# Turning the next expert's rows during the second matrix, in single buffers, with more weight pieces in flight

## The chip, the core and the metric

The kernel runs on one core of one Trainium2 chip. The metric is device time in microseconds (us) of one execution. TensorE (PE) multiplies matrices, VectorE (DVE) and ScalarE (ACT) work elementwise, GpSimd (POOL) issues indirect transfers, and SyncE (SP) issues nearly all the loads of weights. Each engine takes its instructions in the order of its own list.

## What is computed

One decoder layer on 1024 tokens of width 1024. The first third of the time goes to attention and cross-attention; the rest, which the change touches, is the mixture of experts. The router picks 4 of 32 experts for each token, and each expert does this to its tokens:

```python
gu = xb @ w1[e] + b1[e]                          # (rows, 1024) x (1024, 2048)
gate = jnp.minimum(gu[:, :D_FF], SWIGLU_LIMIT)
up = jnp.clip(gu[:, D_FF:], -SWIGLU_LIMIT, SWIGLU_LIMIT)
act = (up + 1.0) * gate * jax.nn.sigmoid(SWIGLU_ALPHA * gate)
return (act @ w2[e] + b2[e]) * g[:, None]        # (rows, 1024) x (1024, 1024)
```

The results are added to the tokens' rows, and a last normalisation follows. All is in float32, so that the 32 experts hold 403 MB of weights.

## The kernel before

**Experts.** The 32 experts are worked one after the other in the fixed `ORDER`. Each has a capacity `CAPS[r]` of rows, the largest rank 204 and the smallest 128. The 18 experts with more than 128 rows go through `ffn_wide`, the 14 with 128 through `ffn_split`; below they are called wide and narrow. Nine times a wide expert follows a narrow one, and 13 of the narrow ones have a successor.

**Weight pieces.** An expert's weights are twelve pieces of 1 MB: eight of the first matrix, four of the second. A piece is loaded on SP's queue as `wt` (768 KB, L1077) and `ww` (256 KB, L1078). `wt` is then split by ACT into a high part `wh` (L1090) and by DVE into a remainder `wl` (L1091); `ww` goes to TensorE as it is. `piece(i, j)` (L1458) sets the order of the program: the splits run four pieces ahead of the matmuls (`AHEAD`), the loads `ahead` pieces ahead. `wt` has 4 buffers, `ww` 6, `wh` and `wl` 6 each. A `wt` buffer is free when its split is done, a `ww` buffer only when TensorE has used the piece. SP's queue is in order, so that a `ww` load that waits for its buffer holds back the `wt` load behind it.

**A wide expert.** For each of four steps `c` in the first matrix, two pieces are multiplied by the turned rows `xT`, `x16`, `xw` (the high and low part, a 16-bit copy, and the part of the rows that is not split) in `packed` (L1134). The result goes through ACT (L1239), DVE (L1241) and the gates to `act`, `a16` and `aw`, which are the operands of the second matrix; `aw` is made by an ACT copy of `ac` (L1232) after the last gate. In the second matrix the first three of four output blocks get their products over the first six of eight parts early (`ek=6`), while the last gates run. `turned` turns the result back through `yT` (L1269), and `scatter` adds it to the rows.

**A narrow expert.** Its rows are the stationary operand (`mm_s`, L1156). `act_T` turns the gated values by TensorE into a `qt` bank in PSUM, and `parted` (L1051) makes the operands from it: `hi` on ACT (L105), `lo` on DVE (L106), the 16-bit copy on ACT (L1061), and the whole part on ACT (L1057). There are two `qt` banks.

**The next expert's rows.** `prep` gathers them from `Hdr` into `xg0` and `xg1` (L1013, POOL's queue), two experts ahead. `x_T` turns them in two to four parts, each through a `qt` bank and `parted`. The parts are spread over the four steps of the first matrix of the expert before (`between`). `xT`, `x16`, `xw` and `xg0` have two buffers each.

**Order.** A scheduler places the instructions of every engine by a simulated timeline, with the priorities `ha` to `hf` in `PLAN`; the code sets only the order of the program.

Of the kernel before, what the change touches and what calls it, by code (L numbers as in the profile page):

```python
# [42 lines left out]
           a16E=1, fb=((0, 1, 2), (3, 4), (5, 6), (7,)), fn=('xg1', 'y1', 'xg0', 'y0', 'xg1', 'y1', 'xg1',  # L43
           'xg0'), tags=0, BB=(3,), avs=(0, 1), PS=(2, 3, 2), LAG=1, AB=2, GB=(2,), ORD3=range(0, 8), m3=28, mulL=0, x16=1, a16=1, a16L=1, early=3, ek=6, prep=3, wt=4, ww=6, wh=6, wl=6, ahead=8,
           gu=2, ac=4)
# [17 lines left out]
def block_kernel(ctx: ExitStack, tc: tile.TileContext, x, mem, win, gcol, grow, wpool, wout, wqT, wkv, wo,  # L63
# [944 lines left out]
    def gather(sb, idx, C):  # L1008
        xg = []
        for g in range((C + P - 1) // P):  # L1010
            m = min(P, C - g * P)
            t = sb.tile([P, D], F32, name=f"xg{g}", bufs=2 - g)
            nc.gpsimd.indirect_dma_start(out=t[:m], out_offset=None, in_=Hdr,  # L1013
                                         in_offset=bass.IndirectOffsetOnAxis(ap=idx[:m, g, 0:1], axis=0))
            xg.append((t, m))
        return xg

    def x_T(sb, q, xg, C):

        if general[0]:  # L1020
            xT = sb.tile([P, KD, P], F32, name="xT")
        else:
            xT, x16, xw = operand(sb, 2 * C, C, "xT", "x16", "xw")
# [70 lines left out]
    def gated(out, g, u, sg):  # L1094

        nc.scalar.activation(sg, g, AF.Silu, scale=ALPHA)
        nc.vector.scalar_tensor_tensor(out, u, 1.0 - LIM, sg, op0=OP.max, op1=OP.mult)
# [111 lines left out]
    def ffn_wide(sb, q, xT, need, r, C, sl, idx, between, last=False):  # L1209

        acts = act, a16, aw = operand(sb, 2 * C, C, "act", "a16", "aw", 1)
        for c in range(4):
# [37 lines left out]
        if last:  # L1250
            fin["rows"] = sb.tile([P, 3, D], F32, name="xT")
            rows = [(fin["rows"][:, g], min(P, C - g * P)) for g in range(2)]
            sq = sq_tile(sb, False)
            for g, (t, m) in enumerate(rows):
                rows_in(idx, g, m, t)
        def finish():
            for eh in range(2):
                for g, (t, m) in enumerate(rows):
                    rows_add(q, sq[:, g, eh:eh + 1], t, ys[g], m, slice(eh * 512, eh * 512 + 512))
            rows_norm(sb, sq, rows)  # L1260
            for g, (t, m) in enumerate(rows):
                rows_out(idx, g, m, t)
# [14 lines left out]
        for eh in range(2):  # L1277
# [3 lines left out]
            early = {e: packed(q, C, parts, cs(e), acts, None, range(PLAN['ek'])) for e in range(PLAN['early'] if eh == 0 else 0)}  # L1281
            for e in range(4):
                py = packed(q, C, parts, cs(e), acts, early.get(e), range(PLAN['ek'] if e in early else 0, KD))
# [3 lines left out]
                settle()  # L1287
            waiting.append(lambda eh=eh, yT=yT: turned(eh, yT))

    def ffn_split(sb, q, xT, need, r, C, sl, idx, between, last=False):  # L1290
# [37 lines left out]
        if last:  # L1328
            t = fin["rows"][:, 2]
# [15 lines left out]

        products(0, 0)
# [20 lines left out]
    with ExitStack() as es:  # L1367
# [55 lines left out]
        prep(1)  # L1423
        XT[0], parts = x_T(sb, q, XG[0], CAPS[ORDER[0]])
        for f in parts:
            f()
        eid = {}
# [39 lines left out]
        for i in range(NE):  # L1467
# [7 lines left out]
            todo_x = []  # L1475

            def between(c):

                if c == 0 and i + 1 < NE:
                    XT[i + 1], todo_x[:] = x_T(sb, q, XG[i + 1], CAPS[ORDER[i + 1]])  # L1480
                for f in when.get((i, c), []):
                    f()
                if c == PLAN['prep']:
                    if i + 2 < NE:
                        prep(i + 2)
                if i == NE - 2:
                    for b in PLAN["fb"][c]:
                        n = PLAN["fn"][b]
                        t = sb.tile([P, D], F32, name=n, bufs=2 - int(n[-1]))
# [6 lines left out]
                n = -(-len(todo_x) // (4 - c))  # L1496
                for _ in range(n):
                    todo_x.pop(0)()

            if C <= P:  # L1500
                ffn_split(sb, q, XT[i], lambda j: piece(i, j), r, C, *S[i], between, i == NE - 1)
            else:
                ffn_wide(sb, q, XT[i], lambda j: piece(i, j), r, C, *S[i], between, i == NE - 2)
# [107 lines left out]
```

## Time and profile before

| | |
|---|---|
| median of 3 runs | 2386.41 us (2385.89 to 2390.04) |
| profiled execution, its own time | 2396.44 us |
| span of its trace | 2394.8 us |
| mean granted clock of TensorE | 0.97 of full speed |
| TensorE busy | 92% of the span |
| DVE, ACT busy | 66%, 56% |
| mean transfer rate | 230 GB/s |

The profiled execution was 10 us longer than the median. A wait is shown as the idle time of an engine before an instruction, with the instruction or transfer that ended last before it. Idle time of TensorE counts where TensorE is the engine that is busy nearly all the time, which is so in the experts: they run from about 840 us to 2370 us, and 860 to 2345 us is used below as their stretch, without the start and the end.

### The profile page before, as it was taken

What the parts mean: (1) busy time and instruction counts of PE and PEld (TensorE: products, weight loads), DVE (VectorE), ACT (ScalarE), POOL (GpSimd) and SP (SyncE); (2) the same over time, 40 slices, a digit from 0 to 9 for tenths busy, and PEclk for the clock granted to TensorE, in tenths of its full rate; (3) what the DMA queues carried; (4) which work ended last, traced back from release to release, by engine and by line L of the source; (5) the groups of instructions that cost most, each with busy time, mean ns of one, the idle gap of its engine ahead of it and who ended that gap; (6) DMA issues with size and microseconds to landing.
All of it is one profiled execution on the core that took longest, in us unless ns stands there. A gap on an engine that the chain in (4) does not pass through costs nothing. (4 is left out here: it accounts for less than half of the span.)

```text
span 2394.8 us, 41782 instructions
## 1 busy us (share of the span) xinstructions
PE 2206.8 (92%) x15378; PEld 1858.8 (78%) x15378; DVE 1578.9 (66%) x2843; ACT 1347.7 (56%) x2349; POOL 463.0 (19%) x389
## 2 busy tenths in 40 slices
PE   8999998889899899999989999999988999899975
PEld 7989886689899767767988588666986887866962
DVE  5742878764755677677766676667667666666675
ACT  6733665433542365666666566666666656665653
POOL 2101566544340010111100111100011101101001
PEclk9999999899999899999999999999999999999998
DMA  7821113154322398889887987988888788799685
GB/s 249 276 87 53 45 45 88 58 161 168 112 89 98 112 337 285 301 313 331 284 277 250 349 311 266 314 292 317 284 274 303 276 282 296 254 323 310 229 296 185
DMA packets 155620, 549.74 MB, mean 230 GB/s; under 512 B 20453, under 2 KB 24677, under 8 KB 152721
## 3 DMA queue, kind: packets, MB, share of 16 engines
q1 hardware_dynamic: 129024, 478.73, 56.7%
q0 software_dynamic: 16032, 46.21, 7.7%
q10 hardware_dynamic: 10354, 22.06, 2.6%
q8 instruction: 124, 2.03, 0.3%
q14 instruction: 86, 0.70, 0.1%
HBM read 493.16 MB, written 49.57 MB: 227 GB/s over the span
## 5 line engine op out<-in xcount | busy, mean ns | idle before, releaser
L1091 DVE SCALAR_TENSOR_TENSOR wl<-wt,wh 128x1536 f16<-128x1536 f32 x384 | 674.6, 1757 | 422.6 <-ACT wh L1090 413.8
L1090 ACT ACTIVATE wh<-wt 128x1536 fp32r<-128x1536 f32 x384 | 569.5, 1484 | 375.5 <-DMA wt<-w 363.2
L1152 PE MATMUL qh<-xT,wh 128*128 128x332 f32 (+17 forms) x1728 | 320.1, 319 | 9.6 <-DVE gu L1241 4.8
L1118 POOL DMA_INDIRECT Adr<-y,idx x50 | 98.8, 1975 | 1005.8 <-ACT y L1270 567.9
L1152 PEld LDWEIGHTS qh<-xT,wh 128*128 128x128 f32 x1728 | 251.4, 189 | 13.3 <-DVE gu L1241 6.2
L1152 PEld LDWEIGHTS <-wl 128*128 128x128 f16 x2592 | 196.3, 99 | 51.3 <-issue 36.0
L1163 PE MATMUL qh<-wh,xT 128*128 128x512 f32 x336 | 205.0, 610 | 0.2 <-ACT wh L1090 0.2
L1152 PE MATMUL qh<-xw,ww 128*128 128x166 f32 (+17 forms) x1152 | 197.0, 293 | 0.0
L1152 PE MATMUL qh<-act,wh 128*128 128x332 f32 (+17 forms) x864 | 182.5, 333 | 9.9 <-DVE gu L1241 4.9
L1152 PEld LDWEIGHTS qh<-xw,ww 128*128 128x128 f32 x1152 | 170.4, 190 | 1.7 <-issue 1.4
L99 PE MATMUL pd<-uhi,Thi 128*128 128x256 f32 x576 | 165.9, 288 | 0.7 <-ACT pe L756 0.4
L100 PE MATMUL pd<-ulo,Thi 128*128 128x256 f32 x576 | 164.0, 285 | 0.0
L101 PE MATMUL pd<-uhi,Tlo 128*128 128x256 f32 x576 | 162.8, 283 | 0.0
L1152 PE MATMUL qh<-x,wl 128*128 128x166 f16 (+17 forms) x1728 | 152.8, 230 | 7.7 <-DVE gu L1241 6.3
L1152 PEld LDWEIGHTS qh<-act,wh 128*128 128x128 f32 x864 | 131.0, 194 | 16.6 <-DVE act L1229 8.2
L1152 PE MATMUL qh<-aw,ww 128*128 128x166 f32 (+17 forms) x576 | 115.4, 315 | 21.3 <-ACT aw L1232 21.3
L1164 PE MATMUL qh<-wh,xT 128*128 128x512 f32 x336 | 134.5, 400 | 0.0
L1165 PE MATMUL qh<-wl,x 128*128 128x512 f16 x336 | 131.3, 391 | 1.5 <-DVE wl L1091 1.5
L1013 POOL DMA_INDIRECT xg<-Hdr,idx x50 | 66.3, 1327 | 282.7 <-PE qt L1031 130.5
L1152 PE MATMUL qh<-a,wl 128*128 128x166 f16 (+17 forms) x864 | 93.9, 236 | 22.5 <-ACT a L1061 18.9
L1239 ACT ACTIVATE gu<-qh,b1P 128x166 f32<-128x166 f32 (+17 forms) x288 | 103.4, 377 | 19.5 <-PE qh L1152 19.4
L1166 PE MATMUL qh<-ww,xw 128*128 128x512 f32 x224 | 114.4, 592 | 0.0
(410 smaller groups left out, 5077.9 us busy)
## 6 DMA issues: line engine op xcount, KB each, us to landing
wt<-w SPq DMA_DIRECT2D x382, 768.0 KB
ww<-w SPq DMA_DIRECT2D x382, 256.0 KB
w<-wkv SPq DMA_DIRECT2D x8, 1024.0 KB
uw<-wout SPq DMA_DIRECT2D x16, 512.0 KB
uw<-Mdr SPq DMA_DIRECT2D x16, 512.0 KB
w<-win SPq DMA_DIRECT2D x5, 1024.0 KB
xt<-x SPq DMA_DIRECT2D x8, 512.0 KB
w<-wqT SPq DMA_DIRECT2D x4, 1024.0 KB
```

What stands on the lines that cost most here:

```text
L99: nc.tensor.matmul(ps, whi, mhi, start=start, stop=False, **kw)
L100: nc.tensor.matmul(ps, whi, mlo, start=False, stop=False, **kw)
L101: nc.tensor.matmul(ps, wlo, mhi, start=False, stop=stop, **kw)
L1090: last_a[0] = nc.scalar.activation(hi, t, AF.Copy, scale=WS).ins
L1091: nc.vector.scalar_tensor_tensor(lo, t, WS, hi.bitcast(F32), op0=OP.mult, op1=OP.subtract)
L1118: nc.gpsimd.indirect_dma_start(out=Adr, out_offset=bass.IndirectOffsetOnAxis(ap=idx[:m, g, 1:2], axis=0), in_=ys[:m], in_offset=None, comp ...
L1152: nc.tensor.matmul(o, a, b, start=new and n == 0, stop=n == len(jobs) - 1 and KD - 1 in ks, skip_group_check=True)
L1163: nc.tensor.matmul(ps, xhi[:, n], hi[:, k], start=start and k == 0, stop=False, **kw)
L1164: nc.tensor.matmul(ps, xlo[:, n], hi[:, k], start=False, stop=False, **kw)
L1165: nc.tensor.matmul(ps, x16[:, n], lo[:, k], start=False, stop=False, **kw)
L1166: nc.tensor.matmul(ps, xw[:, h], t1, start=False, stop=stop, **kw)
L1239: nc.scalar.activation(t[:, g, f], ph[:, C:2 * C], AF.Identity, scale=1.0 / WS, bias=b1P[:, 8 * g + j, r:r + 1])
```

## The change

- `x_T` of the next expert is no longer called in the first matrix. `rows_next` creates its tiles in the second matrix: a wide expert does one part after each output block of the first half, a narrow one does one part after its first product, two after the second and one after the third.
- `xT`, `x16`, `xw` and `xg0` get one buffer. The gather of the expert after the next (`prep`) moves behind the whole expert in the program.
- `wt` has 6 buffers, `ww` 11, and the loads are issued ten pieces ahead. `ac` has 3 buffers where it had 4.
- In a wide expert, the last gate of the first matrix writes `aw` directly on DVE, where an ACT copy made it. The early products run in two rounds, over the first four parts and then over the next two (`ek=(4, 6)`).
- The tiles of the last normalisation are taken from other pools.

```diff
-           'xg0'), ... early=3, ek=6, prep=3, wt=4, ww=6, wh=6, wl=6, ahead=8,
-           gu=2, ac=4)
+           'y0'), ... early=3, ek=(4, 6), wt=6, ww=11, wh=6, wl=6, ahead=10,
+           gu=2, ac=3)
...
-            t = sb.tile([P, D], F32, name=f"xg{g}", bufs=2 - g)
+            t = sb.tile([P, D], F32, name=f"xg{g}", bufs=1)
...
-            xT, x16, xw = operand(sb, 2 * C, C, "xT", "x16", "xw")
+            xT, x16, xw = operand(sb, 2 * C, C, "xT", "x16", "xw", 1)
...
+                    if c == 3 and fs.start == 1:
+                        nc.vector.tensor_scalar(t[:, 1, 1], t[:, 1, 1], LIM + 1.0, WS, op0=OP.min, op1=OP.mult)
+                        return gated(aw[:, 1], t[:, 0, 1], t[:, 1, 1], sg[:, 1], WS)
...
-                    if c % 2 and fs.stop == 2:
-                        nc.scalar.activation(aw[:, c // 2], ac[:, 1], AF.Copy, scale=WS)
+                    if c == 1:
+                        nc.scalar.activation(aw[:, 0], ac[:, 1], AF.Copy, scale=WS)
...
-            early = {e: packed(q, C, parts, cs(e), acts, None, range(PLAN['ek'])) for e in range(PLAN['early'] if eh == 0 else 0)}
+            early, done = {}, 0
+            if eh == 0:
+                todo_x = rows_next()
+                for k in PLAN['ek']:
+                    for e in range(PLAN['early']):
+                        early[e] = packed(q, C, parts, cs(e), acts, early.get(e), range(done, k))
+                    done = k
...
                 settle()
+                if todo_x:
+                    todo_x.pop(0)()
...
         products(0, 0)
         if not last:
             act_T(3)
+        turn_x(1)
         products(1, 0)
...
+        turn_x(2)
         products(0, 1)
         out_half(0)
+        turn_x(1)
         products(1, 1)
...
-                if c == PLAN['prep']:
-                    if i + 2 < NE:
-                        prep(i + 2)
...
+            if i + 2 < NE:
+                prep(i + 2)
```

What this makes of the engines' lists is shown at three places. The first is SP's queue at the first loads of the second half of the first expert and the first of the second expert; the instructions between that only set registers are left out. In brackets stands what a load waits for: `DMA...` are earlier transfers, `PE` and `DVE` the engines that free its buffer. Before:

```order
L1077 DMA wt<-w 128x1536 [waits DMASW3_49,DVE_49]
L1078 DMA ww<-w 128x512 [waits DMAHW5_49,PE_49]
L1077 DMA wt<-w 128x1536 [waits DMASW5_49,DVE_49]
L1078 DMA ww<-w 128x512 [waits DMAHW7_49,PE_49]
L1077 DMA wt<-w 128x1536 [waits DMAHW0_49,DVE_49]
L1078 DMA ww<-w 128x512 [waits DMAHW1_49,DMASW4_49,PE_49]
```

The same loads in the changed kernel:

```order
L1077 DMA wt<-w 128x1536 [waits DMAHW4_49,DVE_49]
L1078 DMA ww<-w 128x512 [waits DMAHW5_49]
L1077 DMA wt<-w 128x1536 [waits DMAHW6_49,DVE_49]
L1078 DMA ww<-w 128x512 [waits DMAHW7_49]
L1077 DMA wt<-w 128x1536 [waits DMAHW0_49,DMASW2_49,DVE_49]
L1078 DMA ww<-w 128x512 [waits DMAHW1_49]
```

The waits for TensorE are gone from these `ww` loads; in the changed list they come back five pieces later.

The second place is ACT's list at the change from the first to the second matrix in the wide expert with 148 rows. Before:

```order
L1096 ACTIVATE sg<-gu 128x148
L1239 ACTIVATE gu<-qh,b1P 128x148 x2
L1090 ACTIVATE wh<-wt 128x1536
L1228 ACTIVATE act<-ac 128x148
L1061 ACTIVATE a_13757<-ac 128x148
L1090 ACTIVATE wh<-wt 128x1536
L1096 ACTIVATE sg<-gu 128x148
L1090 ACTIVATE wh<-wt 128x1536
L1232 ACTIVATE aw<-ac 128x148
L1285 ACTIVATE yT<-qh 128x148 x5
```

The changed kernel at the same place:

```order
L1096 ACTIVATE sg<-gu 128x148
L1242 ACTIVATE gu<-qh,b1P 128x148
L105 ACTIVATE xT<-qt 128x3x128
L1061 ACTIVATE x_14215<-xT 128x384
L105 ACTIVATE xT<-qt 128x3x128
L1090 ACTIVATE wh<-wt 128x1536
L1231 ACTIVATE act<-ac 128x148
L1061 ACTIVATE a_13760<-ac 128x148
L1061 ACTIVATE x_14215<-xT 128x384
L1057 ACTIVATE xw<-qt 128x128 x2
L1090 ACTIVATE wh<-wt 128x1536
L1294 ACTIVATE yT<-qh 128x148 x7
```

The copy to `aw` with two splits of weights ahead of it is gone, and work for the next expert's rows stands between the last gates.

The third place is TensorE's list where a narrow expert ends and a wide one with 152 rows begins. Weight loads alone are left out. Before, from the last turning of the narrow expert's gated values (L1305):

```order
L1305 MATMUL qt<-ident,ac 128x128 x2
L1031 MATMUL qt<-ident,xg_14982 128x128 x2
L1152 MATMUL qh<-x_14792,wl 128x152
L1152 MATMUL qh<-xT,wh 128x304 x3
L1152 MATMUL qh<-xw,ww 128x152 x2
```

The changed kernel, from the same turning (now L1316) and at the end of the narrow expert:

```order
L1031 MATMUL qt<-ident,xg_14739 128x128 x2
L1166 MATMUL qh<-ww,aw 128x512
L1316 MATMUL qt<-ident,ac 128x128 x2
L1163 MATMUL qh<-wh,act 128x512 x2
L1031 MATMUL qt<-ident,xg_14739 128x128 x4
...
L1031 MATMUL qt<-ident,xg_14741 128x24 x8
L1166 MATMUL qh<-ww,aw 128x512 x2
L1152 MATMUL qh<-x_14952,wl 128x152
```

Before, products of the next expert follow the turning; now products that need the turned values follow it at once, and the next expert's first product comes two matmuls after its last rows are turned.

## Rows read from the trace of the kernel before

**Rows 1.** Busy time by stretch, the experts: length, busy us of PE, PEld, DVE, ACT and POOL, granted clock, busy share of the transfer engines, GB/s.

```profile
860.00:2345.00 1485.00, 1391.42 (x9856) 1126.04 (x9855) 1012.09 (x1653) 930.04 (x1580) 163.11 (x130) 0.98 0.86 294
```

**Rows 2.** What TensorE waited for from 860 to 2345 us: line that waited, what ended the wait, us in total, times, longest.

```profile
PE qh L1152 <- ACT aw L1232: 21.3, 8, 7.1
PE qh L1152 <- DVE gu L1241: 19.4, 21, 2.9
PE qh L1152 <- ACT a L1061: 18.9, 16, 3.5
PE qt L1269 <- DVE yT L1286: 13.0, 8, 3.3
PE qh L1152 <- DVE act L1229: 4.8, 10, 0.8
PE qh L1164 <- DVE act L106: 4.2, 5, 1.2
PE qh L1163 <- ACT act L105: 3.0, 3, 1.8
PE qh L1152 <- ACT wh L1090: 2.7, 1, 2.7
```

**Rows 3.** The same for ACT, DVE and SP's queue, the longest of each.

```profile
ACT wh L1090 <- DMA wt<-w: 355.6, 212, 6.5
...
DVE wl L1091 <- ACT wh L1090: 407.9, 257, 9.4
...
SPq L1078 <- PE qh L1152: 596.7, 128, 13.0
SPq L1078 <- PE qh L1166: 308.9, 124, 10.3
```

**Rows 4.** The timeline of SP, ACT, DVE and TensorE around TensorE's longest wait: start, us, instruction, and in brackets the idle time before it and what ended it.

```profile
1743.43 0.23 SPq L1077 DMA_DIRECT2D wt<-w  x1
...
1749.20 0.33 SPq L1077 DMA_DIRECT2D wt<-w  x1
...
1757.37 1.48 ACT L1090 ACTIVATE wh<-wt 128x1536 fp32r<-128x1536 f32 x1 [4.12 <-DMA wt<-w]
1762.40 1.48 ACT L1090 ACTIVATE wh<-wt 128x1536 fp32r<-128x1536 f32 x1 [3.55 <-DMA wt<-w]
1763.79 0.30 ACT L1232 ACTIVATE aw<-ac 128x134 f32<-128x134 f32 x1
...
1760.56 0.29 DVE L1097 SCALAR_TENSOR_TENSOR ac<-gu,sg 128x134 f32<-128x134 f32 x1
...
1764.14 0.81 PE L1152 MATMUL qh<-aw,ww 128*128 128x134 f32 x2 [7.08 <-ACT aw L1232]
```

**Rows 5.** Busy time by stretch around the same wait, columns as in rows 1.

```profile
1750.00:1755.00 5.00, 4.86 (x60) 4.55 (x59) 4.92 (x12) 3.24 (x8) 0.00 (x0) 1.00 1.03 348
...
1760.00:1765.00 5.00, 0.86 (x4) 0.79 (x5) 1.94 (x3) 1.69 (x2) 0.00 (x0) 0.54 0.44 178
1765.00:1770.00 5.00, 5.00 (x41) 4.78 (x40) 3.58 (x8) 3.07 (x8) 0.00 (x0) 0.77 0.24 75
```

**Rows 6.** The timeline of ACT and TensorE where a narrow expert's last gated values are turned, columns as in rows 4.

```profile
968.31 1.48 ACT L1090 ACTIVATE wh<-wt 128x1536 fp32r<-128x1536 f32 x1 [3.38 <-DMA wt<-w]
969.70 0.47 ACT L105 ACTIVATE act<-qt 128x384 fp32r<-128x384 f32 x1
...
970.23 0.73 PE L1163 MATMUL qh<-wh,act 128*128 128x512 f32 x2 [1.81 <-ACT act L105]
972.11 0.80 PE L1164 MATMUL qh<-wh,act 128*128 128x512 f32 x1 [1.16 <-DVE act L106]
```

**Rows 7.** Busy time by stretch directly behind these two waits, columns as in rows 1.

```profile
972.00:976.00 4.00, 3.89 (x11) 2.11 (x11) 4.00 (x7) 2.99 (x5) 0.00 (x0) 0.58 0.84 310
```

**Rows 8.** Groups of ACT's instructions by line from 860 to 2345 us: count, busy us, mean ns of one, idle time before them.

```profile
L1061 ACT ACTIVATE x<-xT 128x384 f16<-128x384 f32 (+9 forms) x80 | 37.7, 473 | 1.1
L105 ACT ACTIVATE xT<-qt 128x384 fp32r<-128x384 f32 (+9 forms) x80 | 34.7, 435 | 11.5 <-PE qt L1031 11.5
...
L1057 ACT ACTIVATE xw<-qt 128x128 f32<-128x128 f32 (+9 forms) x80 | 20.3, 256 | 29.3 <-DVE xT L106 29.2
L1342 ACT ACTIVATE y<-qh,sl 128x512 f32<-128x512 f32 x26 | 17.5, 682 | 12.1 <-PE qh L1166 12.1
L1061 ACT ACTIVATE a<-act 128x384 f16<-128x384 f32 x26 | 13.5, 520 | 0.1
L105 ACT ACTIVATE act<-qt 128x384 fp32r<-128x384 f32 x26 | 12.4, 478 | 6.8 <-PE qt L1305 6.8
L1232 ACT ACTIVATE aw<-ac 128x166 f32<-128x166 f32 (+17 forms) x36 | 11.5, 320 | 2.7 <-DVE ac L1097 2.7
L1057 ACT ACTIVATE aw<-qt 128x128 f32<-128x128 f32 x26 | 7.0, 269 | 1.9 <-DVE act L106 1.9
```

**Rows 9.** The timeline of TensorE in a narrow expert: one round of three matmuls (from one L1165 to the next), and two matmuls of the unsplit part of a piece; columns as in rows 4.

```profile
1378.58 0.39 PE L1165 MATMUL qh<-wl,x 128*128 128x512 f16 x1
...
1379.28 0.39 PE L1165 MATMUL qh<-wl,x 128*128 128x512 f16 x1
1379.51 1.02 PE L1166 MATMUL qh<-ww,xw 128*128 128x512 f32 x2
```

**Rows 10.** The page's transfer issues: the gathers, with their count and the median us from issue to landing.

```profile
xg<-Hdr,idx POOLq DMA_INDIRECT x50, 9.2
```

More of the change, by code (lines that the diff above doesn't have):

```diff
@@ L42 @@
 PLAN = dict(un=2, bgd=((0, 0), (3, 0)), bgt=0, bgp=0, ha=30, hb=100, hc=100, hd=300, he=30, hf=300, mp=26, mq=(26, 27),
-           a16E=1, fb=((0, 1, 2), (3, 4), (5, 6), (7,)), fn=('xg1', 'y1', 'xg0', 'y0', 'xg1', 'y1', 'xg1',
-           'xg0'), tags=0, BB=(3,), avs=(0, 1), PS=(2, 3, 2), LAG=1, AB=2, GB=(2,), ORD3=range(0, 8), m3=28, mulL=0, x16=1, a16=1, a16L=1, early=3, ek=6, prep=3, wt=4, ww=6, wh=6, wl=6, ahead=8,
-           gu=2, ac=4)
+           a16E=1, fb=((0, 1, 2), (3, 4), (5, 6), (7,)), fn=('xg1', 'y1', 'y0', 'xg1', 'y0', 'y1', 'xg1',
+           'y0'), tags=0, BB=(3,), avs=(0, 1), PS=(2, 3, 2), LAG=1, AB=2, GB=(2,), ORD3=range(0, 8), m3=28, mulL=0, x16=1, a16=1, a16L=1, early=3, ek=(4, 6), wt=6, ww=11, wh=6, wl=6, ahead=10,
+           gu=2, ac=3)
 TC_ARGS = dict(schedule_with_timeline_sim=True)
@@ L1207, in settle, with ffn_wide @@
             waiting.pop(0)()
-    def ffn_wide(sb, q, xT, need, r, C, sl, idx, between, last=False):
+    def ffn_wide(sb, q, xT, need, r, C, sl, idx, between, rows_next, last=False):
         acts = act, a16, aw = operand(sb, 2 * C, C, "act", "a16", "aw", 1)
@@ L1249, in ffn_wide @@
         ys = [sb.tile([P, D], F32, name=f"y{g}", bufs=2 - g) for g in range(2)]
[L1250 to L1255, printed above, removed]
+        rows = []
         def finish():
@@ L1280, in ffn_wide @@
             cs = lambda e: slice(e * P, e * P + P)
-            early = {e: packed(q, C, parts, cs(e), acts, None, range(PLAN['ek'])) for e in range(PLAN['early'] if eh == 0 else 0)}
+            early, done = {}, 0
[5 more added lines that the diff above has]
+                    done = k
+            elif last:
+                fin["sq"] = sq_tile(sb, False)
+                for g in range(2):
+                    rows.append((sb.tile([P, D], F32, name=f"xg{g}", bufs=1), min(P, C - g * P)))
+                    rows_in(idx, g, rows[g][1], rows[g][0])
             for e in range(4):
-                py = packed(q, C, parts, cs(e), acts, early.get(e), range(PLAN['ek'] if e in early else 0, KD))
+                py = packed(q, C, parts, cs(e), acts, early.get(e), range(done if e in early else 0, KD))
                 with first(PLAN['hc']):
@@ L1287, in ffn_wide, with ffn_split @@
                 settle()
+                if todo_x:
+                    todo_x.pop(0)()
             waiting.append(lambda eh=eh, yT=yT: turned(eh, yT))
-    def ffn_split(sb, q, xT, need, r, C, sl, idx, between, last=False):
+    def ffn_split(sb, q, xT, need, r, C, sl, idx, between, rows_next, last=False):
         sel = sb.tile([96, P], BF, name="sel")[:, :C]
@@ L1328, in ffn_split @@
         if last:
-            t = fin["rows"][:, 2]
+            t = sb.tile([P, D], F32, name="y1", bufs=1)
             rows_in(idx, 0, C, t)
@@ L1344, in out_half, with turn_x @@
                     rows_add(q, sq[:, 0, eh + c:eh + c + 1], t, ys, C, cs)
+        todo_x = rows_next()
+        def turn_x(n):
+            for f in todo_x[:n]:
+                f()
+            del todo_x[:n]
         products(0, 0)
@@ L1422, in block_kernel @@
         prep(0)
-        prep(1)
         XT[0], parts = x_T(sb, q, XG[0], CAPS[ORDER[0]])
@@ L1426, in block_kernel @@
             f()
+        prep(1)
         eid = {}
@@ L1474, in block_kernel, with rows_next @@
                     fin["g"] = bcast_row(sb, grow[4], "g_f")
-            todo_x = []
+            def rows_next():
+                if i + 1 == NE:
+                    return []
+                XT[i + 1], parts = x_T(sb, q, XG[i + 1], CAPS[ORDER[i + 1]])
+                return parts
             def between(c):
-                if c == 0 and i + 1 < NE:
-                    XT[i + 1], todo_x[:] = x_T(sb, q, XG[i + 1], CAPS[ORDER[i + 1]])
                 for f in when.get((i, c), []):
                     f()
-                if c == PLAN['prep']:
-                    if i + 2 < NE:
-                        prep(i + 2)
                 if i == NE - 2:
@@ L1495, in between @@
                         nc.sync.dma_start(out[b * P:(b + 1) * P], t)
-                n = -(-len(todo_x) // (4 - c))
-                for _ in range(n):
-                    todo_x.pop(0)()
             if C <= P:
-                ffn_split(sb, q, XT[i], lambda j: piece(i, j), r, C, *S[i], between, i == NE - 1)
+                ffn_split(sb, q, XT[i], lambda j: piece(i, j), r, C, *S[i], between, rows_next, i == NE - 1)
             else:
-                ffn_wide(sb, q, XT[i], lambda j: piece(i, j), r, C, *S[i], between, i == NE - 2)
+                ffn_wide(sb, q, XT[i], lambda j: piece(i, j), r, C, *S[i], between, rows_next, i == NE - 2)
+            if i + 2 < NE:
+                prep(i + 2)
     general[0] = True
```

12 lines of the change are left out of this document (6 added, 6 removed).

## The prediction

> **What bounds the kernel now.** I read the busy time by stretch first. In the experts TensorE is busy 1391 of 1485 us, the transfer engines 86% of it, DVE 1012 and ACT 930 us [rows 1]. TensorE is the bound, and its 94 idle us and the time at the lower clock are what can be won; no other engine is near it except the transfers, whose 0.86 x 1485 = 1277 us are a floor below it.
>
> Then the waits, to see what ends TensorE's idle time. It hardly ever waits for weights: `wh` ended 2.7 us of it. The large groups are `aw` 21.3, `gu` 19.4, `a` 18.9 and `yT` 13.0 us, all of them work of ACT and DVE on results, at the seams between the two matrices [rows 2]. Yet ACT waited 355.6 us for weights to land, DVE 407.9 us for ACT's splits [rows 3]. The timeline joins the two. In TensorE's longest wait, 7.08 us for `aw`, ACT stood 4.12 and 3.55 us before two splits whose `wt` had been issued 13.9 and 13.2 us earlier (1743.43 and 1749.20); the gate on DVE came behind the first split and its remainder, and `aw`, a copy of 0.30 us, behind the second [rows 4]. The same happens in a narrow expert: 3.38 us for `wt`, then the copy that TensorE waited 1.81 us for [rows 6]. So late weights cost TensorE time not by themselves, but by standing in ACT's in-order list ahead of short work that it needs.
>
> Why they are late: SP's queue stood 597 + 309 = 906 us before `ww` loads that waited for TensorE to free a buffer [rows 3]. The transfers run full until TensorE stops (busy share 1.03), and 10 us later they are idle for three quarters (0.24), because no buffer came free [rows 5]. That is the signature of too few buffers, not of too little bandwidth.
>
> **The change part by part.** All sums are against the profiled execution, 2396.4 us, which lies 10.0 us above the median; I take the same difference off the median.
>
> *Deeper loads.* What can go is the part of TensorE's waits that stands behind a weight load: `aw` 21.3, `yT` 13.0, `wh` 2.7 and `act` on L105 3.0 whole, and half of `gu` and `a` (38.3), since those two also have many short waits; 40.0 + 19.2 = 59 us. The bounds are the rows that the timeline shows directly, 27 us (`aw`, `wh`, L105), and all eight rows, 87 us [rows 2]. How much of it goes depends on whether the transfers can get ahead. Less its loss by the clock (30 us, next), TensorE needs 1391 - 30 = 1361 us and the transfers 1277 us [rows 1], a surplus of 84 us over 32 experts, 2.6 us each. A piece is 1277 / 384 = 3.3 us of transfers, so the lead grows by less than a piece per expert, and the first third of the experts gets little of it. I take 80%: -47 us, with a third (-20) and all (-59) as bounds.
>
> The Trainium skill (Perfetto Trace Analysis, section Identifying the Most-Contended Engine, with the peak of its section Engine Utilization) judges transfers not by busy time but against 358 GB/s for a core. By that, the 294 GB/s of the row would leave a floor of 1220 us and a surplus of 141, the lead would fill sooner, and this term would be about -52; the rows' busy share is the stricter measure, and I keep it.
>
> *Clock.* The mean of 0.98 over 1485 us is 30 us lost [rows 1], 22 to 37 by its rounding; it falls where TensorE stood, 0.54 and 0.77 behind the wait of 7 us [rows 5]. The loss goes with the long waits, so I take three quarters: -22.
>
> *`aw` on DVE, early products in two rounds.* 18 copies of 0.32 us leave ACT [rows 8]; the waits for `aw` are counted above. Three more blocks of products now stand before the first use of the last parts but one, which covers the other half of `a` (9.5) and `act` on L1229 (4.8) [rows 2]. I take 6 of these 14 us, bounds 0 and 14.
>
> *Turning the next rows in the second matrix.* The work is the same, and in a wide expert it lies between products that wait for gates anyway. A narrow expert loses cover. Before, the next expert's first products follow the last `act_T`; now they cannot, since their rows are not yet turned. The list on ACT after the turning of `xg` is `xT` 0.435, `x16` 0.473, then `act` 0.478, together 1.39 us [rows 8], against one matmul of 0.51 [rows 9] and two transposes on TensorE: 0.4 to 0.9 us are open. The next transposes need the `qt` bank that `a` 0.520, `xw` 0.256 and `aw` 0.269 hold, 1.05 us, against two matmuls of 0.73 together [rows 6, 8]. I take 1.2 us, 13 times: +16. At the nine seams from narrow to wide, the last `xT` 0.435, an output copy 0.682 and `x16` 0.473 make 1.59 us [rows 8] against two matmuls of 1.02 [rows 9]; with the hand-overs 1.0 us, nine times: +9. The nearest row for either kind is the pair of 1.81 and 1.16 us [rows 6], which bounds both at 2.97 us, 65 us in all; below they are bounded by nothing. That pair brought the clock to 0.58 for 4 us [rows 7], a loss of 1.7 us, and my shorter waits should do that at three of 13 experts: +5, with 22 as the bound. Together +30, from 0 to 87.
>
> The skill's page TensorE: Matmul & The Clock Gate (section HAM oscillation) ties the lower clock to idle gaps longer than the gate's own window, by which none of my new waits would cost clock, and the last term would be +25. The two waits of the row, neither of them as long as that, did cost it, so I keep +30.
>
> *No cost taken.* A gather lands 9.2 us after its issue [rows 10]. It is now issued when the rows before it are turned, in one second matrix, and wanted in the next, behind eight pieces; for a narrow expert these are eight times 3 x 0.70 + 0.51 = 2.6 us [rows 9], 21 us. If that cover were gone, every expert would wait for the rest. `ac` with three buffers is reused three steps later, when it has been read. The start has four pieces on the way before the first split and now six; the end hangs on the scatters as before.
>
> Sum: -47 - 22 - 6 + 30 = -45. 2396.4 - 45 = 2351 profiled, **2341 as the median**.
>
> **Rivals.**
>
> *The lead fills at once.* All waits behind loads (-59), all of the clock (-30), all 14 of the third term, and half of the new costs (+15): -88, 2298. For it: one wide expert frees the queue at once, and 906 us of SP's waiting is a large reserve [rows 3]. Against: the surplus of 2.6 us an expert.
>
> *Bandwidth is the limit.* The loads took 13.9 and 13.2 us in a queue that was full [rows 4, 5], and each load still waits for a transfer four pieces before it, as the list of the changed SP queue shows; if the pieces come no sooner, only a quarter of the first two terms goes: -15 - 7 - 6 + 30 = +2, 2388. This is also the case that the change does not do what it says. Against it is the share of 0.24 behind the wait [rows 5].
>
> *Slower: ACT falls behind in the narrow experts.* Their second matrix is 4 x 2.6 = 10.4 us on TensorE [rows 9]. ACT now has four splits of 1.48 [rows 4], one set for `act` (0.478 + 0.520 + 0.269), two output copies of 0.682 and up to four parts of 0.435 + 0.473 + 0.256 [rows 8]: 5.9 + 1.3 + 1.4 + 4.7 = 13.2 us. The parts have the priority, so the splits slip by up to 3 us per narrow expert. The four pieces of lead (10 us) should absorb that; if they don't, it costs 13 x 3 = 39 us and the clock at each hand-over, 22, beside the 25: 86 - 75 = +11, 2397. The change is slower once a hand-over costs over 75 / 13 = 5.8 us, waits and clock together.
>
> **How the numbers follow.** The forecast, 2318 to 2365 by its own bounds, has 0.53; the lead that fills at once 0.20; bandwidth 0.16; ACT behind 0.11. A measurement can tell about 0.2%, 5 us, from no change. Faster holds the first two and a quarter of the third: 0.77; same, half of the third: 0.08; slower, the rest of it and the fourth: 0.15. The range is 2298 to 2388: it leaves out the fourth case and the lower tail of the second.
>
> **What would show it.** In the changed profile: ACT's wait for `wt` well below 355.6 us, mostly in the first third of the experts; SP waiting for DVE's splits in place of TensorE; hardly any `aw` group among TensorE's waits, and `yT` below 5 us; a mean clock of 0.99 in the experts; new waits of 1 to 2 us for L105 and L106 at each narrow expert, and for L1061 at the first product behind it; a transfer share above 0.88. I am wrong if ACT still waits over 200 us for `wt`, or if waits at the ends of the narrow experts come to more than 65 us.

## The result, and the profile after

| | before | after |
|---|---|---|
| median of 4 runs each | 2388.22 us (2385.89 to 2390.24) | 2315.0 us (2312.57 to 2317.5) |
| ratio, 95% interval | | 0.9694 [0.9676, 0.9712] |
| profiled execution | 2396.44 us | 2312.57 us |
| span of its trace | 2394.8 us | 2311.0 us |

The changed kernel is 3.1% faster, 73 us by the medians and 84 us between the two profiled executions. The forecast was 45. The medians below are over all runs; the ratios leave out three slow executions of 3684 to 7535 us, one of the kernel before and one each of two of the kernels below.

The busy time by stretch, from 860 us to TensorE's last matmul, first of the kernel before and then of the changed one:

```profile
860.00:2367.00 1507.00, 1412.73 (x9938) 1137.36 (x9936) 1031.07 (x1691) 941.75 (x1599) 167.64 (x133) 0.98 0.85 293
```

```profile
860.00:2285.00 1425.00, 1389.83 (x9933) 1124.03 (x9931) 1036.24 (x1692) 949.33 (x1582) 161.50 (x133) 0.99 0.89 309
```

The stretch is 82 us shorter. TensorE's idle time, the first number less the second, fell from 94.3 to 35.2 us: 59 us. The other 23 us are busy time, 1412.73 and 1389.83 us for nearly the same number of matmuls. The clock, 0.98 and then 0.99, gives about 16 of them (0.02 x 1507 - 0.01 x 1425); each of the two terms has some 7 us of rounding, so the rest can be clock too, which these rows don't decide. ACT's busy time did not fall, 941.75 and 949.33 us: what changed is when it works.

What ended TensorE's waits in the changed kernel (total, times, longest), as [rows 2] showed it before:

```profile
PE qt L1267 <- DVE yT L1295: 10.3, 3, 7.2
PE qt L1316 <- DVE ac L1097: 5.1, 3, 2.4
PE qh L1163 <- ACT act L105: 3.5, 6, 0.6
...
PE qh L1152 <- DVE gu L1244: 3.2, 4, 1.4
PE qh L1152 <- ACT x L1061: 3.0, 6, 1.1
PE qh L1164 <- DVE act L106: 1.7, 3, 1.3
PE qt L1031 <- ACT xw L1057: 1.5, 3, 0.9
...
PE qh L1152 <- ACT a L1061: 1.0, 2, 0.6
```

(The lines have moved a little: the products' results are now read on L1242 and L1244, `act` is made on L1231 and L1232, `yT` on L1294 and L1295.) The group `aw` is gone, `gu` fell from 19.4 to 3.2 and `a` from 18.9 to 1.0. The waits for the operands that the turning of the next rows feeds or stands before are those for L105, L106, L1061 and L1057, 9.7 us together, beside 0.7 us for `xT` on L106; what it delays further back in the lists is not counted by this. 7.2 of the 10.3 us of `yT` are one wait near the end, which has a part of its own below.

The waits behind these, on ACT, DVE and SP's queue, which answer to [rows 3]:

```profile
ACT gu L1242 <- PE qh L1152: 153.4, 135, 3.5
ACT wh L1090 <- PE qh L1164: 108.7, 109, 3.2
...
ACT wh L1090 <- DMA wt<-w: 0.8, 3, 0.3
...
DVE wl L1091 <- ACT wh L1090: 160.8, 139, 7.5
...
SPq L1077 <- DVE wl L1091: 296.4, 164, 4.0
SPq L1078 <- PE qh L1152: 287.9, 105, 7.8
```

ACT's wait for weights went from 355.6 us to 0.8. It now waits for TensorE: for results to read, and for `wh` buffers to come free. That is what an engine off the critical path should wait for. The two lines of SP's queue are alike, but a `wt` load waits under other lines of DVE too. By its groups of over 5 us the queue stands 522 us before `wt` loads, for DVE to free a buffer, and 399 us before `ww` loads, for TensorE; the second was 961 us in the kernel before.

When the lead filled is read from the 40 us ahead of the experts and their first 80 us, before and then after (share of the transfer engines and GB/s are the last two columns), and from ACT's waits from 840 to 1100 us in the kernel before:

```profile
800.00:840.00 40.00, 30.40 (x252) 25.52 (x252) 26.88 (x113) 12.88 (x31) 6.20 (x9) 0.73 0.44 159
840.00:880.00 40.00, 37.76 (x171) 21.52 (x169) 30.77 (x43) 25.05 (x36) 6.98 (x6) 0.93 0.96 338
880.00:920.00 40.00, 40.00 (x317) 36.24 (x318) 31.47 (x45) 29.50 (x50) 2.44 (x1) 1.00 0.92 322
```

```profile
800.00:840.00 40.00, 28.73 (x227) 22.64 (x226) 23.99 (x105) 10.74 (x27) 6.42 (x10) 0.67 0.53 194
840.00:880.00 40.00, 37.17 (x159) 20.87 (x158) 33.45 (x42) 27.97 (x33) 0.99 (x1) 0.90 0.96 370
880.00:920.00 40.00, 38.90 (x312) 35.31 (x310) 31.27 (x46) 28.15 (x48) 3.73 (x3) 1.00 0.98 356
```

```profile
ACT wh L1090 <- DMA wt<-w: 53.4, 33, 5.1
```

At nearly the same busy share the changed kernel moved 363 GB/s over the 80 us, the one before 330, and in the 40 us ahead of them 194 against 159. That is 4 MB, or four pieces, more by 920 us, 1.4 MB of them before 840. By 840 us, before its first split (841.59), the changed kernel had issued six `wt` loads, four on SP's queue from 822.35 us on and two on POOL's; the one before had issued the fourth only at 840.10 us. The higher rate is one of the start: over the whole stretch above, both move about the same for their busy share, 293 GB/s at 0.85 and 309 at 0.89. The lead was there from the first experts on: ACT's 0.8 us for `wt` are those of the whole stretch from 860 us, where the kernel before had 53.4 us by 1100.

### The profile page after: what moved, and what is told of

It reads as the page before. It is cut to its first block, busy times and chain, and to the rows that moved or that the text cites. A ratio compares the mean times of both kernels' runs of the same rounds, so it can differ in the third digit from the quotient of the medians.

```text
span 2311.0 us, 41986 instructions
## 1 busy us (share of the span) xinstructions
PE 2182.1 (94%) x15378; PEld 1842.2 (80%) x15378; DVE 1586.9 (69%) x2843; ACT 1356.7 (59%) x2331; POOL 456.5 (20%) x389
## 5 line engine op out<-in xcount | busy, mean ns | idle before, releaser
L1091 DVE SCALAR_TENSOR_TENSOR wl<-wt,wh 128x1536 f16<-128x1536 f32 x384 | 667.9, 1754 | 191.6 <-ACT wh L1090 163.1
L1090 ACT ACTIVATE wh<-wt 128x1536 fp32r<-128x1536 f32 x384 | 562.0, 1480 | 137.0 <-PE qh L1164 108.7
L1242 ACT ACTIVATE gu<-qh,b1P 128x166 f32<-128x166 f32 (+17 forms) x288 | 104.9, 381 | 154.2 <-PE qh L1152 153.4
L1152 PE MATMUL qh<-act,wh 128*128 128x332 f32 (+17 forms) x864 | 175.6, 328 | 4.4 <-DVE act L1232 3.2
L1152 PE MATMUL qh<-x,wl 128*128 128x166 f16 (+17 forms) x1728 | 146.4, 229 | 4.8 <-ACT x L1061 3.0
L1244 DVE SCALAR_TENSOR_TENSOR gu<-qh,gu 128x166 f32<-128x166 f32 (+17 forms) x288 | 81.6, 311 | 83.1 <-ACT gu L1242 82.2
L1165 PE MATMUL qh<-wl,x 128*128 128x512 f16 x336 | 131.7, 392 | 0.6 <-DVE wl L1091 0.6
L598 POOL TENSOR_TENSOR ulo<-uw,uhi 128x1024 fp32r<-128x1024 f32 x36 | 88.8, 2476 | 122.9 <-ACT uhi L597 113.6
```

The lines of the kernel that those rows point to most:

```text
L1090: last_a[0] = nc.scalar.activation(hi, t, AF.Copy, scale=WS).ins
L1091: nc.vector.scalar_tensor_tensor(lo, t, WS, hi.bitcast(F32), op0=OP.mult, op1=OP.subtract)
L1152: nc.tensor.matmul(o, a, b, start=new and n == 0, stop=n == len(jobs) - 1 and KD - 1 in ks, skip_group_check=True)
L1165: nc.tensor.matmul(ps, x16[:, n], lo[:, k], start=False, stop=False, **kw)
L1242: nc.scalar.activation(t[:, g, f], ph[:, C:2 * C], AF.Identity, scale=1.0 / WS, bias=b1P[:, 8 * g + j, r:r + 1])
```

## The experiments

Theory A is the one that the result suggests: the depth of the loads is what pays, because a late `wt` stands ahead of short work in ACT's list, and `ww` is the buffer that held SP's queue. The rivals: (B) taking the turning out of the first matrix pays by itself; (C) `aw` and the early products pay by themselves. The kernel before took 2383.18, 2378.79 and 2380.17 us on the three chips used; each ratio is to the kernel before on its own chip.

| kernel | median us | ratio, 95% |
|---|---|---|
| changed, old depth | 2429.45 | 1.0186 [1.014, 1.0232] |
| changed, `ww` 6 | 2444.37 | 1.0289 [1.0254, 1.0325] |
| before, `ww` 9 | 2360.72 | 0.9905 [0.9872, 0.9939] |
| changed, `wt` 3, `ww` 9 | 2397.0 | 1.0074 [1.0045, 1.0103] |
| the same, two buffers for the rows | 2390.98 | 1.0037 [1.0012, 1.0061] |
| before, `aw` on DVE | 2375.12 | 0.9965 [0.9937, 0.9993] |
| before, two rounds | 2377.35 | 0.9988 [0.9969, 1.0008] |
| changed, no `aw`, one round | 2345.79 | 0.9832 [0.9801, 0.9864] |
| changed, one round | 2344.35 | 0.9841 [0.981, 0.9871] |
| changed, three rounds | 2341.05 | 0.9829 [0.9801, 0.9858] |
| changed, blocks earlier | 2318.11 | 0.9735 [0.9709, 0.9762] |
| changed, blocks in other tiles | 2321.93 | 0.9754 [0.9727, 0.978] |

**All but the depth.**

```diff
-wt=6, ww=11, wh=6, wl=6, ahead=10
+wt=4, ww=6, wh=6, wl=6, ahead=8
```

> The changed kernel with the buffers and the lead of before (wt 4, ww 6, eight ahead); the turning in the second matrix, aw on DVE and the two early rounds stay. Theory (the deeper loads are the gain): ACT waits over 250 us for wt again, and the time is 2370 to 2400 us. Rival (the gain is the turning's new place, or aw and the early rounds): 2315 to 2335 us, with ACT's wait for wt still small.

Measured: 2429.45 us, slower than the kernel before by 1.86%, or 44 us, and above what was expected. So rival B falls: without the buffers, the rest of the change costs. With them the ratio is 0.9694; the depth is worth 0.0492 of 2383 us, 117 us, in this arrangement. The waits of this kernel:

```profile
ACT wh L1090 <- DMA wt<-w: 382.9, 217, 6.4
...
SPq L1078 <- PE qh L1152: 630.1, 123, 16.3
...
PE qt L1031 <- DMA xg<-Hdr,idx: 21.4, 4, 7.4
```

The old picture is back, and a new group with it: gathers that land late. The timeline of POOL and TensorE around one of them:

```profile
1392.71 2.11 POOL L1013 DMA_INDIRECT xg<-Hdr,idx  x1 [27.14 <-PE qt L1031]
...
1400.86 1.08 PE L1031 MATMUL qt<-ident,xg 128*128 128x128 f32 x4 [5.91 <-DMA xg<-Hdr,idx]
```

The gather into the single `xg0` waited 27.14 us in POOL's list until TensorE had turned the rows before. TensorE has the first part of the next rows early in its own list, and waited 5.91 us for them.

**Which buffer held the loads.**

```diff
-wt=6, ww=11, wh=6, wl=6, ahead=10
+wt=6, ww=6, wh=6, wl=6, ahead=10
```

> The changed kernel with ww back at 6 buffers; wt stays at 6 and the loads at ten pieces ahead in the program. Theory A (ww was the holder, since it is free only when the TensorE has used the piece, and SP's queue is in order): ACT waits for wt 300 us or more again, SP stands before ww for TensorE, and the time is 2390 to 2430, near the 2429 of the kernel with all three old depths. Theory B (the wt buffers or the distance in the program held the loads): ACT's wait stays below 100 us and the time near 2320 to 2335.

Measured: 2444.37 us, above the range expected and at least as slow as with all three old depths. ACT and SP in this kernel:

```profile
ACT wh L1090 <- DMA wt<-w: 389.4, 218, 7.0
...
SPq L1078 <- PE qh L1152: 650.7, 125, 17.2
```

Six `wt` buffers and ten pieces of distance in the program are worth nothing while `ww` has six: SP stands before `ww`, and the `wt` loads behind it. Theory A holds as to the holder. (Four `wt` buffers with eleven of `ww` were not run.)

**More `ww` in the kernel before**, in the room that a `wt` buffer leaves.

```diff
-wt=4, ww=6, wh=6, wl=6, ahead=8
+wt=3, ww=9, wh=6, wl=6, ahead=7
```

> The kernel before with ww 9 and wt 3, seven ahead: the same room, no part of the change but that ww no longer holds SP's queue. Theory (the early stop of SP's in-order queue at ww is the cause): most of the gain without moving anything, 2320 to 2350 us, ACT's wait for wt below 120 us. Rival (it needs the larger lead in wt, and so the room that single buffers give): 2370 to 2395 us.

Measured: 2360.72 us, 22 faster. ACT's wait for `wt` fell to

```profile
ACT wh L1090 <- DMA wt<-w: 235.3, 159, 4.4
```

with fewer pieces ahead in the program than before. About a third of the gain was to be had with no other change; the time lies between the two that were expected. The wait for `wt` did not go further because the holder has changed: SP's queue now stands before `wt` loads, for the splits to free one of three buffers.

```profile
SPq L1077 <- DVE wl L1091: 488.3, 142, 10.2
```

**The changed kernel at that depth**, so that it differs from the last one in the turning with its single buffers, `aw`, the rounds and the smaller parts of the change, and not in the depth.

```diff
-wt=6, ww=11, wh=6, wl=6, ahead=10
+wt=3, ww=9, wh=6, wl=6, ahead=7
```

> The changed kernel with the depth of the earlier experiment on the kernel before (wt 3, ww 9, seven ahead), which took 2360.7 us. The two differ in the turning, the single buffers, aw and the early rounds, not in the depth. If the turning in the second matrix costs what I forecast (+30, less what aw and the rounds give, 6 to 31), it takes 2360 to 2385. If the turning in single buffers costs only where weights are late, as with the old depth (+46 over the kernel before), it lies between: 2345 to 2365, and its late gathers are fewer than the 21.4 us there.

Measured: 2397.0 us, above both ranges expected; the two ratios differ by 0.0169, 40 us. TensorE's waits in this kernel, of which the last three groups were 5.1, 3.5 and 1.7 in the changed kernel over nearly the same stretch:

```profile
PE qt L1267 <- DVE yT L1295: 29.2, 6, 7.8
PE qt L1316 <- DVE ac L1097: 13.5, 9, 6.5
PE qh L1163 <- ACT act L105: 10.8, 8, 3.2
PE qh L1164 <- DVE act L106: 8.6, 9, 1.2
```

So what comes with the turning has no constant cost: 40 us where ACT waits 213.5 us for weights, and some 10 us of waits of its own where ACT waits for none. Gathers are not what costs here; they end 1.0 us of TensorE's waits.

**Is it the place or the single buffers?** The last kernel, with two buffers again for `xT`, `x16`, `xw` and `xg0`:

```diff
-xT, x16, xw = operand(sb, 2 * C, C, "xT", "x16", "xw", 1)
+xT, x16, xw = operand(sb, 2 * C, C, "xT", "x16", "xw")
...
-t = sb.tile([P, D], F32, name=f"xg{g}", bufs=1)
+t = sb.tile([P, D], F32, name=f"xg{g}", bufs=2 - g)
...
```

> The changed kernel with few weight buffers (wt 3, ww 9, seven ahead) and, in the room this leaves, two buffers again for xT, x16, xw and xg0; the rows are still turned in the second matrix. The same with single buffers took 2397.0 us. Theory A (the place of the turning costs: its work stands among the splits and output copies of the second matrix, and makes these late when there is little lead): double buffers give at most 10 us, 2387 to 2400. Theory B (the single buffers cost, by late gathers and by turned rows that wait until their buffer is read): 2355 to 2375, near the 2360.7 of the kernel before at this depth.

Measured: 2390.98 us, by the ratios 0.0037 or 9 us less than the last kernel, and the two intervals overlap. So the buffers are not most of the 40 us. That the place is, is argued and not shown: the scheduler's order, which can differ between these kernels too, moves the changed kernel by over 30 us further below. The 117 us of the depth are well beyond that.

**`aw` alone, and two rounds alone, in the kernel before.**

```diff
+if c == 3 and fs.start == 1:
+    nc.vector.tensor_scalar(t[:, 1, 1], t[:, 1, 1], LIM + 1.0, WS, op0=OP.min, op1=OP.mult)
+    return gated(aw[:, 1], t[:, 0, 1], t[:, 1, 1], sg[:, 1], WS)
...
-if c % 2 and fs.stop == 2:
-    nc.scalar.activation(aw[:, c // 2], ac[:, 1], AF.Copy, scale=WS)
+if c == 1:
+    nc.scalar.activation(aw[:, 0], ac[:, 1], AF.Copy, scale=WS)
```

> The kernel before with aw of the last gate written on DVE, and nothing else of the change. Theory (the waits for aw are waits behind loads, and the gate on DVE stands behind the same splits): 2375 to 2388 us. Rival (the ACT copy is what TensorE waits for): 2355 to 2368 us, the 21 us of aw gone.

Measured: 2375.12 us, 8 less. The second one:

```diff
-early=3, ek=6
+early=3, ek=(4, 6)
...
```

> The kernel before with the early products of the second matrix in two rounds (first four parts, then the next two), and nothing else. With the changed kernel's depth the second round was worth 35 us (2344 against 2315). Theory A (the round gives TensorE work that does not wait for the last gates but one, at any depth): 2350 to 2370 here. Theory B (it pays only when the gates, not the loads, are the last to arrive): within 8 us of the kernel before.

Measured: 2377.35 us, no difference that can be told. Rival C falls for the kernel before.

**Both undone in the changed kernel**, and then **one round** with `aw` left on DVE, and **three**:

```diff
-if c == 3 and fs.start == 1: ... gated(aw[:, 1], ...)
...
-ek=(4, 6)
+ek=(6,)
```

> The changed kernel with aw made by the ACT copy again and the early products in one round over six parts. Theory (once weights are early, the copy stands behind nothing that waits): 2313 to 2325 us. Rival (the copy and the round themselves were a large part of TensorE's waits): 2335 us or more, with aw among TensorE's waits at over 10 us.

```diff
-ek=(4, 6)
+ek=(6,)
```

> The changed kernel with the early products in one round over the first six parts, as before the change; aw stays on DVE. Without both, the changed kernel took 2345.8 us, 31 more than with both. Theory A (the round matters: with early weights the TensorE reaches the second matrix while the gates of the last step still run, and needs work that depends on fewer of them): most of the 31 us comes back here, 2330 to 2345, with more TensorE waits for a, act on L1229 and L105. Theory B (the copy of aw on ACT was what held the seams): 2315 to 2322 here.

```diff
-ek=(4, 6)
+ek=(2, 4, 6)
```

> The changed kernel with three rounds of early products, over parts 0 to 1, 2 to 3 and 4 to 5. If the gain of the second round is that TensorE is less often held by one late part, a third gives a little more, 2308 to 2315. If two rounds already cover the gates, no change, 2312 to 2320; if it is the order that the scheduler makes of it, anything between 2310 and 2345.

Measured: 2345.79, 2344.35 and 2341.05 us, by the ratios all three are 32 to 35 us above the changed kernel, and not to be told from each other. So it is not `aw`, and not the number of rounds: one and three are alike. Nor is it the lead: ACT waits 0.8 to 2.0 us for `wt` in all three, and the wait for `aw` where it is undone is 0.7 us, not the 10 that were expected. What is left is the order that the scheduler makes, which two rounds happened to turn out well. The traces show two places. The first is the seam between the matrices in the wide expert with 137 rows. In the changed kernel, DVE's last gate but one and what ACT does after it:

```profile
1444.62 0.43 DVE L1097 SCALAR_TENSOR_TENSOR ac<-gu,sg 128x274 f32<-128x274 f32 x1
...
1445.37 1.49 ACT L1090 ACTIVATE wh<-wt 128x1536 fp32r<-128x1536 f32 x1
1446.76 0.42 ACT L1231 ACTIVATE act<-ac 128x274 fp32r<-128x274 f32 x1
```

The same in the kernel with one round, with TensorE's waits and, in the last two rows, the two stretches of 7 us from 1462 us:

```profile
1459.90 0.44 DVE L1097 SCALAR_TENSOR_TENSOR ac<-gu,sg 128x274 f32<-128x274 f32 x1
...
1459.95 1.48 ACT L1090 ACTIVATE wh<-wt 128x1536 fp32r<-128x1536 f32 x1 [0.43 <-PE qh L1152]
1461.34 0.85 ACT L105 ACTIVATE xT<-qt 128x384 fp32r<-128x384 f32 x2
1462.08 1.48 ACT L1090 ACTIVATE wh<-wt 128x1536 fp32r<-128x1536 f32 x1
1463.45 0.43 ACT L1231 ACTIVATE act<-ac 128x274 fp32r<-128x274 f32 x1
...
1464.26 0.28 PE L1152 MATMUL qh<-a,wl 128*128 128x137 f16 x2 [2.10 <-ACT a L1061]
...
1466.23 0.59 PE L1152 MATMUL qh<-act,wh 128*128 128x274 f32 x1 [1.14 <-DVE act L1232]
...
1462.00:1469.00 7.00, 3.76 (x21) 3.28 (x20) 6.43 (x11) 5.93 (x14) 0.00 (x0) 0.69 1.02 388
1469.00:1476.00 7.00, 7.00 (x72) 6.69 (x71) 3.97 (x14) 2.75 (x6) 0.00 (x0) 0.82 0.29 110
```

In the changed kernel `act` comes 1.71 us after the gate, behind one split. With one round the next rows' `xT` and a second split stand ahead of it, and it comes 3.11 us after. TensorE waited 2.10 and 1.14 us, and the clock was 0.69 and then 0.82, at most 2.2 and 1.3 us lost. The kernels with three rounds and with neither have the same order and nearly the same delay there, 3.12 us each. From DVE's first work on the results of the wide expert before this one to its first on those of the narrow one behind, the two wide experts take 92.1 us in the changed kernel, 97.9 with one round and 97.6 with three. The four wide experts with 158, 140, 130 and 148 rows take 182.4, 189.5 and 191.6 by the same measure; in the one with 140 rows, `act` comes 2.62 us after the gate in the changed kernel, behind two splits, and 3.26 in the other two, behind two splits and `xT`. These two stretches hold 13 to 15 of the 32 to 35 us. That this order is the cause was not tried by itself.

The second place is the end: from TensorE's last matmul to the end of the span it is 25.7 us in the changed kernel, 38.4 with one round, 38.7 with three, 36.8 with neither. What stands behind it came out with the last pair.

**The longest wait that is left.** In the last wide expert, TensorE waits 7.25 us for `yT`. Eight blocks of the final normalisation are worked in between there; they are loaded (L1510), squared on ACT (L1169), scaled and written out (L1515), in tiles that they share with the rows (`fn`). ACT and the clock in the changed kernel:

```profile
2221.21 0.60 ACT L1169 ACTIVATE qs<-y 128x512 f32<-128x512 f32 x1 [3.24 <-DMA y<-Adr]
...
2223.82 1.24 ACT L1294 ACTIVATE yT<-qh 128x204 f32<-128x204 f32 x5
...
2228.00:2238.00 10.00, 10.00 (x50) 9.50 (x51) 6.72 (x29) 2.98 (x9) 0.11 (x1) 0.71 0.92 334
```

ACT waited 3.24 us before a square, whose block was still loading, and did `yT` behind it; DVE, which waited 2.43 us for the same square's sums, did two remainders, 3.42 us, ahead of its own part of `yT`. It is the pattern of [rows 4] with another load. Two attempts to remove it:

```diff
-fb=((0, 1, 2), (3, 4), (5, 6), (7,))
+fb=((0, 1, 2, 3), (4, 5), (6, 7), ())
```

> The changed kernel with the squares and sums of the final normalisation's blocks taken an expert earlier. In the changed kernel the TensorE's longest wait behind 860 us, 7.25 us for yT in a wide expert near the end, stands behind ACT's square of such a block, which waited 3.24 us for its rows. If the place of that block is the cause, the wait goes, with the 10 us at the lower clock behind it: 2303 to 2310. If the block is as late at its new place, or a like wait comes elsewhere, no change or a few us more: 2313 to 2325.

Measured: 2318.11 us, a ratio of 0.9735, no better; the wait was 9.5 us. The second:

```diff
-fb=((0, 1, 2), (3, 4), (5, 6), (7,)), fn=('xg1', 'y1', 'y0', 'xg1', 'y0', 'y1', 'xg1', 'y0')
+fb=((0, 1, 2, 3), (4, 5), (6,), (7,)), fn=('xg1', 'y1', 'y0', 'y0', 'xg1', 'y1', 'xg1', 'y0')
```

> The changed kernel with the tiles of the final normalisation's blocks in another order: the fourth block takes the second y0 buffer and the fifth xg1, so that the load of the fourth does not wait for the first block to be written out. The longest wait of TensorE behind 860 us, 7.25 us for yT near 2220 us, stood behind a square on ACT that waited 3.24 us for the fifth block's load. If the shared tile made that load late, the wait goes with its 10 us at the lower clock: 2302 to 2311. If it stands behind weight loads on SP's queue whatever its tile: 2313 to 2323.

Measured: 2321.93 us, not the 2302 to 2311 expected with the wait gone, although the wait went (the longest for `yT` is 2.7 us) and TensorE ended at 2282.4 instead of 2285.3 us. (The edit also takes some blocks a step earlier, as the first attempt did, where the wait stayed.) The end took 37.9 us instead of 25.7. POOL's list and SP's write of the last `xg` block, in the changed kernel:

```profile
2242.76 0.35 SPq L1515 DMA_DIRECT2D out<-xg  x1
...
2249.91 3.02 POOL L1187 DMA_INDIRECT xg<-Adr,idx  x1 [12.77 <-DVE rs_a L131]
2259.01 2.64 POOL L1118 DMA_INDIRECT Adr<-y,idx  x1 [6.09 <-issue]
...
2279.58 1.02 POOL L1187 DMA_INDIRECT y<-Adr,idx  x1 [9.39 <-issue]
```

and with the other tiles:

```profile
2258.05 0.35 SPq L1515 DMA_DIRECT2D out<-xg  x1
...
2261.70 1.16 POOL L1187 DMA_INDIRECT xg<-Adr,idx  x1 [14.25 <-DVE act L106]
2269.85 2.31 POOL L1118 DMA_INDIRECT Adr<-y,idx  x1 [7.00 <-issue]
...
2288.88 1.02 POOL L1187 DMA_INDIRECT y<-Adr,idx  x1 [9.16 <-issue]
```

The last wide expert reads its rows back into the same `xg1` tile. The block in it was written out 15 us later, so the read-back came 12 us later, and in POOL's in-order list the two scatters and the last expert's read-back stood behind it. With one round the same write went out at 2288.13 us and the read-back at 2291.75, with three rounds at 2285.77 and 2289.44, with neither at 2283.30 and 2286.92. So the timelines show one mechanism behind the 11 to 13 us at the end in all four, a shared tile ahead of a chain of transfers on POOL; no run changed this tile alone. No version was found that beats the changed kernel.

## Why the prediction came out as it did

The direction and the main mechanism held: late weights cost time through ACT's list, and buffers, not bandwidth, made them late. The forecast of 2341 was 26 us too high, and its own bounds (2318 to 2365) just missed 2315. These bounds don't follow from those of the terms, of which the turning alone had 0 to 87. What came is closest to the rival "the lead fills at once", 2298, to which I gave 0.20. Yet a part of the 26 us is luck: with one or three rounds, or without `aw` and the rounds, and with the same lead, the kernel takes 2341 to 2346 us, just the forecast. The 32 to 35 us below that come with an order of the lists that the prediction did not look at, so the time itself says little on how well the terms were sized; the waits say more.

- *Deeper loads, forecast -47.* This term was too small, and one step in it failed: "the lead grows by less than a piece per expert, and the first third of the experts gets little of it". By 920 us, in the second expert, the changed kernel had moved four pieces more than the one before, and ACT hardly waited for `wt` from then on. The prediction has the larger start as a remark ("four pieces on the way before the first split and now six") and gives it no part in the lead; and its mean surplus over 32 experts, 2.6 us each, says nothing of the start, where the transfers ran at 363 GB/s. The price of a piece did not fail: over the whole stretch its busy time is 3.3 us in both kernels (0.85 x 1507 / 384 and 0.89 x 1425 / 384). The Trainium skill (Perfetto Trace Analysis, section Engine Utilization) puts the peak for a core at 358 GB/s, which by its note a core that works alone can pass; the trace shows 370 over 40 us, so the figure was no limit here. By that figure the estimate for this term was -52, a little nearer. Of the waits that I counted, `aw`, `wh`, `gu` and `a` fell from 62.3 to 4.2 us, half of the last two being too little; `yT` fell only from 13.0 to 10.3, and L105 not at all (3.0 and 3.5).
- *Clock, forecast -22.* About -16 by the mean, within the rounding; with the +5 for the new waits the forecast was -17 in all.
- *`aw` and two rounds, forecast -6.* At the old depth they give 8 and 3 us by themselves, the second not to be told from none. In the changed kernel undoing the rounds, with or without `aw`, costs 32 to 35 by the ratios, but by the order of ACT's list at two seams and by the end, not by the cover that I argued from. The term was not just too small: the reason given for it is not what the runs show. That the order of the lists is the reason fits the traces, and was not tried by itself.
- *Turning in the second matrix, forecast +30.* The size was near what all but the depth costs at little depth (40 at `wt` 3 and `ww` 9; 44 at the old depth). At full depth the waits for it come to 9.7 us, and none of the clock's +5 is seen from 980 to 2220 us, where the granted clock is 1.00. I added this term to the first as if the two were independent. The runs speak against that: the same work costs little once there is lead. That it is the slipping splits that cost is my reading of the lists.
- *No cost taken for the gathers.* Right at full depth, where no such wait is among the groups behind 860 us; at the old depth it was 21.4 us, because a gather into the single buffer is issued only once the rows before are turned, and these were turned late.
- *Slower, because ACT falls behind.* Without the buffers the kernel is indeed slower, 2429 us at the old depth, but not by this rival: ACT has time left there, 382.9 us of waits for weights, so the loads are late and not ACT.
- *What would show it.* ACT's wait for `wt`, the `aw` group, the clock of 0.99 and the share of 0.89 came as written. `yT` stayed above 5 us by one wait near the end. SP waits more for the splits than for TensorE, as forecast, though 399 us of the second are left. The new waits of 1 to 2 us at each narrow expert did not come: L105 has six, the longest 0.6 us, and L106 three.

## What to carry to other kernels

Look which buffer the in-order queue of loads stands before: raising the others does nothing, as six `wt` buffers did nothing with six of `ww`. Ask how many pieces are on the way before the first is used, and what rate the start gets, before spreading a mean surplus over all stages. Costs of moved work and gains of lead are not added: first ask what the moved work costs once there is lead. And where a scheduler sets the order, a small edit (one round, two, three) can move the time by 30 us through lists that it never names, so compare the lists at the seams before giving the edit a reason.

## What was not expected of the hardware

- The transfers of the changed kernel moved 363 GB/s over the 80 us from 840 us, and those of the kernel with one round 388 over 7 us at a busy share of 1.02. The kernel before moved 330 over the same 80 us, at shares of 0.96 and 0.92. So a busy share near 1 comes with different rates over short stretches, while over the whole stretch the two kernels have the same rate for their share (345 and 347 GB/s, as 293 / 0.85 and 309 / 0.89).
- Around two waits of TensorE, 2.10 and 1.14 us, the kernel with one round had a granted clock of 0.69 and 0.82 of full speed, in the stretches of 7 us with and behind them. The Trainium skill (TensorE: Matmul & The Clock Gate, section HAM oscillation) ties a falling clock to idle gaps longer than the gate's own window; here, as in [rows 7], it fell behind a pair of short waits.
- A chain of indirect transfers on the same rows takes 9 to 11 us a link at the end of the changed kernel: scatter, scatter and read-back are issued at 2259.01, 2268.35 and 2279.58 us. With the blocks in other tiles the links are 8 and 11 us.
